# Weights of three stages in one pool, and the mixer's gate product, sum and split in the PSUM bank

## The chip, the core and the metric

The kernel runs on one core of a Trainium2 chip. The metric is the time of one execution on the device in microseconds (us); each kernel's time is the median of several runs. Engines: TensorE (PE; PEld is its weight load), VectorE (DVE), ScalarE (ACT), GpSimd (POOL) and SyncE (SP), which here issues every DMA.

## The reference, cut to what matters

Two transformer blocks over 1024 positions of width 1024, in fp32. The part that the change touches is the first half of block 1:

```python
h = rms_norm(x, g_pre_mix)
q, k, v, cb, cc, cu, ga, gc = split(h @ w_in)
o = stick_breaking_attention(heads(q), heads(k), heads(v))   # 8 heads of 64
y_attn = o @ w_attn_out
y_conv = (cb * causal_depthwise_conv(cc * cu, w_conv)) @ w_conv_out
gate_attn, gate_conv = split(sigmoid([ga, gc] + b_gate))
mixed = (gate_attn * y_attn + gate_conv * y_conv) @ w_o
x = x + rms_norm(mixed, g_post_mix)
...                          # MLP (relu squared, 4096 wide), a gated addition from p,
...                          # then block 2: two attention layers with memory
```

## The kernel before

Activations lie transposed, features on the 128 partitions, and each fp32 matrix product is three matmuls of a wider type: every operand is split in a high part and the rest, and `mm3` (L120 to L126) adds high by high (L124), low by high (L125) and high by low (L126) into one PSUM bank of 128 x 512. A weight tile comes by `split_w` (L89 to L105): SP loads it raw (L103), ACT makes the high part (L104), POOL the low part (L105). An activation is split by `split` (L107 to L113): ACT the high part (L112), DVE the low part (L113). `proj_T` runs `mm3` over the k tiles for one half of 512 positions.

The stages run in the order of `STAGES`. `start` makes the normed input, the convolution branch and its gate, and stores `gate_conv * y_conv` in memory as `sT` (L595 sigmoid, L598 product into `s_yc`, L599 store). `stick` (L601) is the attention: four pairs of heads, for each the weights of k, v and q; to the later pairs a `gate` (L630 on) is added that makes one of the first seven tiles of `gate_attn` (L637, into `ga`, one buffer) and stores it in `gaT` (L638). Gates 5 and 6 run at its end. The attention output goes to memory as `oT`, high and low part (L647, L648). `mix` (L657) makes the eighth gate (weight `w7`, tile `ga7`), reads `oT` back into `oh4` and `ol4` (L679, L680; 16 loads of 256 KB), and for each of eight tiles `m` of the mixed output loads a `w_attn_out` tile, `gaT[m]` into `ga_m` (L686) and `sT[m]` into `s_m` (L687). For each half it multiplies in PSUM bank `ps_y` (12 matmuls), then on DVE `ga = ps_y * ga` (L692) and `ga = ga + s` (L693), then splits `ga` into `act_hi` and `act_lo` (L112, L113). `ps_y` has six banks. Then `out_stage`, whose first matmuls are `r_o` (L760 to L762), with `w_o` as the weight.

`run` (L70) opens the pools. A stage or tuple of stages that stands in a tuple gets `dense` (L79): a pool `w` with two buffers each of `wraw`, `w_hi` and `w_lo`, and a pool `wx` with four more of each part, to which two of three weights go. `stick` opens a pool `w` of its own, without `wx`. Where a pool closes and the next opens at the same addresses, the tiles of the new one wait until those of the old one are released. The order of instructions on each engine is set by a scheduler, from dependences, buffers and its own estimates, not by the order of the code.

Of the kernel before, what the change touches and what calls it, by code (L numbers as in the profile page):

```python
# [13 lines left out]
ALU = mybir.AluOpType  # L14
# [14 lines left out]
class Net:  # L29
# [40 lines left out]
    def run(self, stages):  # L70

        for s in stages:
            with ExitStack() as st:
                if isinstance(s, tuple):
                    self.dense(st)
                for name in (s if isinstance(s, tuple) else (s,)):
                    getattr(self, name)()


    def dense(self, st):  # L80

        self.weights(st)
        self.wx = st.enter_context(self.tc.tile_pool(name="wx", bufs=4))
        st.callback(lambda: setattr(self, "wx", None))

# [515 lines left out]
    def stick(self):  # L601

        nc, tc, a = self.nc, self.tc, self.a
        hi, lo = self.act_hi, self.act_lo
        act = (hi, lo)
        col = lambda k: slice(k * P, (k + 1) * P)
        bg = self.bg
        gaT = self.gaT = self.dram.tile([8, P, S], F32, name="gaT")
        oT = self.oT = self.dram.tile([4, 2, P, S], F32, name="oT")
        with ExitStack() as st:  # L610
            self.weights(st)
            A = self.attn_pools(st, (3, 0, 3, 1, 1), stick=True)
            Ts = {}

            def produce(p):
                def gen():
                    T = Ts[p] = self.pair_tiles(A, p)
                    for gi, what in ((4, "k"), (8, "v"), (0, "q")):
                        w = self.split_w(a["w_in"][gi + p], 1024)
                        for h in range(2):  # L620
                            ps = self.ps_proj(A)
                            self.proj_T(ps, w, col, act, 8, h)
                            if what == "v":
                                self.v_evac(A, ps, T, h)
                            else:
                                self.qk_evac(ps, h, T, what, 0.125 if what == "q" else None, once=True)
                            yield
                return gen

            def gate(m):  # L630
                def gen():
                    w = self.split_w(a["w_in"][24 + m], 1024)
                    for h in range(2):
                        ps = self.ps_proj(A)
                        self.proj_T(ps, w, col, act, 8, h)
                        s = A["pp"].tile([P, H], F32, name="ga", tag="ga", bufs=1)
                        nc.scalar.activation(out=s, in_=ps, func=AF.Sigmoid, bias=bg[:, m:m + 1])  # L637
                        nc.sync.dma_start(out=gaT[m, :, h * H:h * H + H], in_=s)  # L638
                        yield
                return gen  # L640

            def items_of(p):
                def done(c, op, _):
                    oh = A["pp"].tile([P, H], F32R, name="oh", tag="oh", bufs=1)
                    ol = op.bitcast(F32R)
                    self.split(oh, ol, op)
                    nc.sync.dma_start(out=oT[p, 0, :, c * H:c * H + H], in_=oh.bitcast(F32))  # L647
                    nc.sync.dma_start(out=oT[p, 1, :, c * H:c * H + H], in_=ol.bitcast(F32))  # L648
                return self.pair_items(Ts[p], "stick", None, 1.0, done)

            self.run_pairs(A, [(6, produce(p)) for p in range(4)], items_of,
                           [[], [], [(2, gate(0))], [(2, gate(m)) for m in range(1, 5)]])
            for m in (5, 6):
                for _ in gate(m)():
                    pass

    def mix(self):  # L657

        nc, tc, a = self.nc, self.tc, self.a
        hi, lo = self.act_hi, self.act_lo  # L660
        act = (hi, lo)
        col = lambda k: slice(k * P, (k + 1) * P)
        sT, gaT, oT = self.sT, self.gaT, self.oT
        with ExitStack() as st:
            cv = st.enter_context(tc.tile_pool(name="mxo", bufs=1))
            c2 = st.enter_context(tc.tile_pool(name="mx2", bufs=4))
            psm = st.enter_context(tc.tile_pool(name="psmx", bufs=6, space=PSUM))
            oh = cv.tile([P, 4, S], F32R, name="oh4")
            ol = cv.tile([P, 4, S], F32R, name="ol4")
            w7 = self.split_w(a["w_in"][31], 1024)  # L670
            w0 = self.split_w(a["w_attn_out"][0], 512)
            ga7 = cv.tile([P, S], F32, name="ga_7")
            for h in range(2):
                sl = slice(h * H, h * H + H)
                ps = psm.tile([P, H], F32, name="ps_y")
                self.proj_T(ps, w7, col, act, 8, h)
                nc.scalar.activation(out=ga7[:, sl], in_=ps, func=AF.Sigmoid, bias=self.bg[:, 7:8])
                for p in range(4):
                    nc.sync.dma_start(out=oh[:, p, sl].bitcast(F32), in_=oT[p, 0, :, sl])  # L679
                    nc.sync.dma_start(out=ol[:, p, sl].bitcast(F32), in_=oT[p, 1, :, sl])  # L680
            for m in range(8):
                w = self.split_w(a["w_attn_out"][m], 512) if m else w0
                ga = c2.tile([P, S], F32, name="ga_m") if m < 7 else ga7
                s = c2.tile([P, S], F32, name="s_m")
                if m < 7:
                    nc.sync.dma_start(out=ga, in_=gaT[m])  # L686
                nc.sync.dma_start(out=s, in_=sT[m])  # L687
                for h in range(2):
                    sl = slice(h * H, h * H + H)
                    ps = psm.tile([P, H], F32, name="ps_y")  # L690
                    self.proj_T(ps, w, col, (oh, ol), 4, h)
                    nc.vector.tensor_tensor(out=ga[:, sl], in0=ps, in1=ga[:, sl], op=ALU.mult)  # L692
                    nc.vector.tensor_tensor(out=ga[:, sl], in0=ga[:, sl], in1=s[:, sl], op=ALU.add)  # L693
                    self.split(hi[:, m, sl], lo[:, m, sl], ga[:, sl])


    def out_stage(self, wsrc, gpost, gpre, xsrc, xdst, filler=None, after=None, first=(), banks=None):
# [876 lines left out]
                self.out_stage(a["w_out_2"][1], a["norm_post_2"][1:2], None, self.xd, self.a["out"], first=first)  # L1574


STAGES = (("start",), "stick", ("mix", "mlp", "layer_a"), "attn_a", "layer_b")


@with_exitstack  # L1580
def tile_net(ctx: ExitStack, tc: tile.TileContext, args: dict):
    Net(ctx, tc, args).run(STAGES)

# [82 lines left out]
```

## Time and profile before

| | us |
|---|---|
| median of 3 runs | 2939.25 (2936.12 to 2941.45) |
| the profiled execution | 2939.78 |
| its span | 2938.0 |
| mean granted clock of TensorE, of full speed | 0.979 |

In a row of the timeline stand the start in us, the duration, the engine, the line of the kernel, the operation and `out<-in`; in square brackets how long the engine had been idle before it and what ended that. Matmul durations overlap: one of 0.39 us starts 0.23 us after the last at full clock, one of 0.63 us 0.43 us after the last at the lower clock. A row with `xN` covers N instructions in a row.

### The profile page before, as it was taken

How to read it: one execution, taken by the hardware profiler on the slowest of the kernel's cores; microseconds unless marked ns; L12 is line 12 of the kernel's file. 1: busy time of each engine (PE TensorE's matmuls, PEld its weight loads, DVE VectorE, ACT ScalarE, POOL GpSimd, SP SyncE). 2: the span in 40 equal slices, each digit the busy share in tenths (PEclk: the TensorE clock that was granted, in tenths of full speed). 3: DMA queues.
4: the chain of work that ended last, by engine and by line, in shares of the span. 5: the costliest groups of instructions: out<-in, count | busy, mean ns of one | idle time of the engine just before them, and what ended most of it. 6: DMA issues, size and time to landing. Idle time of an engine off the chain costs nothing. (4 is left out here: it accounts for less than half of the span.)

```text
span 2938.0 us, 37990 instructions
## 1 busy us (share of the span) xinstructions
PE 2767.0 (94%) x13490; PEld 2303.1 (78%) x13490; DVE 1684.0 (57%) x3177; ACT 1222.8 (42%) x2403; POOL 985.6 (34%) x826
## 2 busy tenths in 40 slices
PE   7999999997999999999989899699999999999988
PEld 5888778886887887888867789677777988788867
DVE  5420288855387766766577534377872436666643
ACT  5111266643352222211134423377773535555542
POOL 4211111113235543222246312332324344555441
PEclk9999999998999999999999999899999999999999
DMA  5112211117323335332123321543344332222163
GB/s 208 47 43 68 75 46 60 58 61 251 118 97 106 128 109 170 115 105 93 66 71 136 133 94 64 180 122 95 121 137 170 106 117 65 72 72 74 56 204 118
DMA packets 140293, 311.15 MB, mean 106 GB/s; under 512 B 15868, under 2 KB 35964, under 8 KB 140104
## 3 DMA queue, kind: packets, MB, share of 16 engines
q1 hardware_dynamic: 140104, 308.73, 31.4%
q8 instruction: 107, 1.75, 0.2%
q14 instruction: 82, 0.67, 0.1%
HBM read 213.33 MB, written 85.38 MB: 102 GB/s over the span
## 5 line engine op out<-in xcount | busy, mean ns | idle before, releaser
L105 POOL TENSOR_TENSOR w_lo<-w_raw,w_hi 128x1024 fp32r<-128x1024 f32 (+5 forms) x223 | 440.2, 1983 | 1036.0 <-ACT w_hi L104 1021.5
L104 ACT ACTIVATE w_hi<-w_raw 128x1024 fp32r<-128x1024 f32 (+5 forms) x223 | 193.0, 877 | 407.3 <-PE ps L125 90.6
L124 PE MATMUL ps_m<-act_hi,w_hi 128*128 128x512 f32 x716 | 287.2, 401 | 22.6 <-DVE qb L343 6.3
L125 PE MATMUL ps_m<-act_lo,w_hi 128*128 128x512 f32 x716 | 281.4, 393 | 0.0
L126 PE MATMUL ps_m<-act_hi,w_lo 128*128 128x512 f32 x716 | 280.7, 393 | 0.2
L113 DVE TENSOR_TENSOR pl<-tp_at,ph 128x512 fp32r<-128x512 f32 (+3 forms) x416 | 222.9, 561 | 84.0 <-ACT ph L112 81.8
L112 ACT ACTIVATE ph<-tp_at 128x512 fp32r<-128x512 f32 (+3 forms) x416 | 196.7, 500 | 107.6 <-PE tp_at L304 96.4
L304 PE MATMUL tp_at<-ident,p 128*128 128x128 f32 x1280 | 204.9, 275 | 18.0 <-DVE pl L113 6.5
L259 ACT ACTIVATE p<-p,mx 128x256 f32<-128x256 f32 (+7 forms) x256 | 180.2, 706 | 74.5 <-DVE mx L248 41.6
L1037 DVE TENSOR_TENSOR acc<-ps_d,acc 128x512 f32<-128x512 f32 x240 | 161.5, 687 | 82.1 <-PE ps_d L126 82.1
L124 PE MATMUL ps_d<-w_hi,act_hi 128*128 128x512 f32 x512 | 200.3, 391 | 2.8 <-DVE f_out L890 1.3
L125 PE MATMUL ps_d<-w_lo,act_hi 128*128 128x512 f32 x512 | 199.5, 390 | 0.0
L126 PE MATMUL ps_d<-w_hi,act_lo 128*128 128x512 f32 x512 | 199.5, 390 | 0.0
L304 PEld LDWEIGHTS tp_at<-ident,p 128*128 128x128 f32 x1280 | 152.6, 141 | 50.6 <-DVE pl L113 9.2
L124 PEld LDWEIGHTS ps_m<-act_hi,w_hi 128*128 128x128 f32 x716 | 135.3, 189 | 58.3 <-PE s_ps L226 8.8
L760 PE MATMUL r_o<-w_hi,act_hi 128*128 128x512 f32 x384 | 152.0, 399 | 12.4 <-DVE ga L692 8.0
L126 PEld LDWEIGHTS ps_m<-act_hi,w_lo 128*128 128x128 f32 x716 | 134.7, 188 | 29.3 <-POOL w_lo L105 1.3
L125 PEld LDWEIGHTS ps_m<-act_lo,w_hi 128*128 128x128 f32 x716 | 135.3, 189 | 25.5
L296 PE MATMUL o_ps<-ph,v 128*128 128x512 f32 (+3 forms) x400 | 146.5, 367 | 6.3 <-ACT ph L112 3.3
L762 PE MATMUL r_o<-w_hi,act_lo 128*128 128x512 f32 x384 | 151.9, 396 | 0.0
L761 PE MATMUL r_o<-w_lo,act_hi 128*128 128x512 f32 x384 | 151.6, 396 | 0.0
L297 PE MATMUL o_ps<-pl,v 128*128 128x512 f32 (+3 forms) x400 | 147.6, 377 | 0.4 <-DVE pl L113 0.2
(393 smaller groups left out, 6930.1 us busy)
## 6 DMA issues: line engine op xcount, KB each, us to landing
w_raw<-in_w_in SPq DMA_DIRECT2D x40, 512.0 KB, 3.5
w_raw<-in_w_up SPq DMA_DIRECT2D x32, 512.0 KB, 3.6
f_rows_up<-f_out SPq DMA_DIRECT2D x64, 256.0 KB, 2.4
f_raw<-f_rows_up SPq DMA_DIRECT2D x64, 256.0 KB, 2.6
w_raw<-in_w_down SPq DMA_DIRECT2D x32, 512.0 KB, 4.5
xd<-x_o SPq DMA_DIRECT2D x16, 512.0 KB, 2.8
x_o<-xd SPq DMA_DIRECT2D x16, 512.0 KB, 10.6
w_raw<-in_w_out SPq DMA_DIRECT2D x13, 512.0 KB, 5.2
```

What stands on the lines that cost most here:

```text
L104: nc.scalar.activation(out=hi[:, sl], in_=raw, func=AF.Copy)
L105: nc.gpsimd.tensor_tensor(out=lo[:, sl], in0=raw, in1=hi[:, sl].bitcast(F32), op=ALU.subtract)
L112: nc.scalar.activation(out=hi, in_=src, func=AF.Copy)
L113: nc.vector.tensor_tensor(out=lo, in0=src, in1=hi.bitcast(F32), op=ALU.subtract)
L124: nc.tensor.matmul(out, lhsT=sh, rhs=mh, start=(i == 0), stop=False)
L125: nc.tensor.matmul(out, lhsT=sh, rhs=ml, start=False, stop=False)
L126: nc.tensor.matmul(out, lhsT=sl, rhs=mh, start=False, stop=(i == n - 1))
L259: nc.scalar.activation(out=p[:, :nk], in_=p[:, :nk], func=AF.Exp, scale=-1.0, bias=mx[:, 0:1], accum_out=it["sum"][:, j:j + 1])
L304: nc.tensor.transpose(tp[:, j * P:(j + 1) * P], it["p"][j][:, k * P:(k + 1) * P], self.ident)
L760: nc.tensor.matmul(r, lhsT=a, rhs=wh, start=(k == 0), stop=False)
L762: nc.tensor.matmul(r, lhsT=b, rhs=wh, start=False, stop=(k == 7))
L1037: nc.vector.tensor_tensor(out=acc[:, t, sl], in0=ps, in1=acc[:, t, sl], op=ALU.add)
```

## The change

`STAGES` nests `start`, `stick` and the tuple `("mix", "mlp", "layer_a")` in one tuple, and `run` opens the pool `w` once for it. `stick` no longer opens one. `wx` is opened by the new `ahead` for an inner tuple alone, so for `start` and for `mix` to `layer_a`, as before. In `mix`, product and sum are written to the bank `ps` and the split reads it; `ga` and `s` are only read. The number of instructions of each kind and engine stays the same.

```diff
@@ run
                 if isinstance(s, tuple):
-                    self.dense(st)
-                for name in (s if isinstance(s, tuple) else (s,)):
-                    getattr(self, name)()
+                    self.weights(st)
+                for d in (s if isinstance(s, tuple) else (s,)):
+                    with ExitStack() as more:
+                        if isinstance(d, tuple):
+                            self.ahead(more)
+                        for name in (d if isinstance(d, tuple) else (d,)):
+                            getattr(self, name)()
@@ dense
         self.weights(st)
+        self.ahead(st)
+
+    def ahead(self, st):
         self.wx = st.enter_context(self.tc.tile_pool(name="wx", bufs=4))
@@ stick
         with ExitStack() as st:
-            self.weights(st)
             A = self.attn_pools(st, (3, 0, 3, 1, 1), stick=True)
@@ mix
-                    nc.vector.tensor_tensor(out=ga[:, sl], in0=ps, in1=ga[:, sl], op=ALU.mult)
-                    nc.vector.tensor_tensor(out=ga[:, sl], in0=ga[:, sl], in1=s[:, sl], op=ALU.add)
-                    self.split(hi[:, m, sl], lo[:, m, sl], ga[:, sl])
+                    nc.vector.tensor_tensor(out=ps, in0=ps, in1=ga[:, sl], op=ALU.mult)
+                    nc.vector.tensor_tensor(out=ps, in0=ps, in1=s[:, sl], op=ALU.add)
+                    self.split(hi[:, m, sl], lo[:, m, sl], ps)
@@ end
-STAGES = (("start",), "stick", ("mix", "mlp", "layer_a"), "attn_a", "layer_b")
+STAGES = ((("start",), "stick", ("mix", "mlp", "layer_a")), "attn_a", "layer_b")
```

Lines of the changed kernel are numbered 7 higher from `dense` to `stick`, 6 higher from there on: L104 is L111, L113 is L120, L692 is L698.

The order moves at three places. ACT from `start` to `stick` (`s_yc` is the last work of `start`; `ka` is the first result of `stick`; each `w_hi` here is a weight of `stick`), before:

```order
L595 ACTIVATE s_yc<-ps,bg 128x512 x6
L104 ACTIVATE w_hi<-w_raw 128x1024 x2
L337 ACTIVATE ka_2110<-ps_m_2119 128x512
L104 ACTIVATE w_hi<-w_raw 128x1024
L337 ACTIVATE ka_2110<-ps_m_2150 128x512
```

and now:

```order
L602 ACTIVATE s_yc<-ps,bg 128x512 x3
L111 ACTIVATE w_hi<-w_raw 128x1024
L602 ACTIVATE s_yc<-ps,bg 128x512 x3
L111 ACTIVATE w_hi<-w_raw 128x1024
L344 ACTIVATE ka_2106<-ps_m_2115 128x512
L111 ACTIVATE w_hi<-w_raw 128x1024
```

The first weight of `stick` stands three activations earlier; its load on SP and its L105 on POOL have moved with it.

SP from `stick` to `mix` (`oT` and `gaT` are the stores of `stick`; `in_w_in` the weight `w7`), before:

```order
L638 DMA gaT<-ga 128x512 x2
L647 DMA oT<-oh 128x512
L648 DMA oT<-opair 128x512
L638 DMA gaT<-ga 128x512
L103 DMA w_raw<-in_w_in 128x1024
L103 DMA w_raw<-in_w_attn_out 128x512
L638 DMA gaT<-ga 128x512
L679 DMA oh_5409<-oT 128x512
L680 DMA ol_5410<-oT 128x512
```

and now (the load of `w7` stands five rows ahead of these):

```order
L644 DMA gaT<-ga 128x512 x2
L653 DMA oT<-oh 128x512
L654 DMA oT<-opair 128x512
L110 DMA w_raw<-in_w_attn_out 128x512 x2
L644 DMA gaT<-ga 128x512
L110 DMA w_raw<-in_w_attn_out 128x512 x3
L644 DMA gaT<-ga 128x512
L110 DMA w_raw<-in_w_attn_out 128x512
L685 DMA oh_5401<-oT 128x512
L686 DMA ol_5402<-oT 128x512
```

Seven of eight `w_attn_out` loads stand before the first `oh` load, one of them before these rows; before it was one of eight, and the other seven stood among the loads of `ga_m` and `s_m`. On PE the 48 `w7` matmuls, which stood behind the last gate, now stand 23 between its halves and 25 behind it.

DVE at the end of `mix` (`ga_5423` is `ga7`; L777 is the first work on `r_o`), before:

```order
L692 TENSOR_TENSOR ga_m<-ps_y,ga_m 128x512
L693 TENSOR_TENSOR ga_m<-ga_m,s_m 128x512
L113 TENSOR_TENSOR act_lo<-ga_m,act_hi 128x512 x2
L692 TENSOR_TENSOR ga_5423<-ps_y,ga_5423 128x512
L693 TENSOR_TENSOR ga_5423<-ga_5423,s_m 128x512
L113 TENSOR_TENSOR act_lo<-ga_5423,act_hi 128x512
L692 TENSOR_TENSOR ga_5423<-ps_y,ga_5423 128x512
L693 TENSOR_TENSOR ga_5423<-ga_5423,s_m 128x512
L113 TENSOR_TENSOR act_lo<-ga_5423,act_hi 128x512
```

and now:

```order
L120 TENSOR_TENSOR act_lo<-ps_y,act_hi 128x512
L699 TENSOR_TENSOR ps_y<-ps_y,s_m 128x512
L698 TENSOR_TENSOR ps_y<-ps_y,ga_5415 128x512
L120 TENSOR_TENSOR act_lo<-ps_y,act_hi 128x512
L699 TENSOR_TENSOR ps_y<-ps_y,s_m 128x512
L120 TENSOR_TENSOR act_lo<-ps_y,act_hi 128x512
L783 TENSOR_TENSOR r_5854<-r_o,gpost 128x512 x8
```

The three passes of a tile are the same; the last product now stands ahead of the split of the tile before it. The last reader of a `ps_y` bank is now the split.

The lists also differ at the tail of the MLP (1490 to 1680 us of the trace), where the down projection's rows are normed (`rstd_y`), scaled (L1012, L991) and transposed on PE (`tp`, split by L112 and L113), and the gate matmuls `ps_pg` run. ACT there, before:

```order
L1004 ACTIVATE junk_f,ss<-acc 128x1024 x2
L112 ACTIVATE act_hi<-tp 128x4x128
L1012 ACTIVATE acc<-acc,rstd_y 128x512
L991 ACTIVATE xn<-acc,rstd_y 128x512
L112 ACTIVATE act_hi<-tp 128x4x128
L104 ACTIVATE w_hi<-w_raw 128x1024
```

and now:

```order
L1010 ACTIVATE junk_f,ss<-acc 128x1024 x2
L119 ACTIVATE act_hi<-tp 128x4x128 x2
L111 ACTIVATE w_hi<-w_raw 128x1024
L1018 ACTIVATE acc<-acc,rstd_y 128x512
L997 ACTIVATE xn<-acc,rstd_y 128x512
L1056 ACTIVATE g_p<-ps_pg 128x512
```

The second split of the pair and one weight stand ahead of the scaling that follows `rstd_y`.

## Rows read from the trace of the kernel before

**Rows 1.** The page, part 1: busy time of each engine, share of the span, instructions.

```profile
PE 2767.0 (94%) x13490; PEld 2303.1 (78%) x13490; DVE 1684.0 (57%) x3177; ACT 1222.8 (42%) x2403; POOL 985.6 (34%) x826
```

**Rows 2.** Timeline of PE, start to stick: start us, us, operation, [idle before <-releaser].

```profile
324.73 0.79 PE L124 MATMUL ps_m<-act_hi,w_hi 128*128 128x512 f32 x1 [5.61 <-ACT w_hi L104]
...
328.73 0.57 PE L124 MATMUL ps_m<-act_hi,w_hi 128*128 128x512 f32 x1
329.14 0.40 PE L125 MATMUL ps_m<-act_lo,w_hi 128*128 128x512 f32 x1
```

**Rows 3.** Timeline of the other engines at the same place.

```profile
319.19 0.81 SPq L103 DMA_DIRECT2D w_raw<-in_w_in  x2
319.23 0.69 DVE L598 TENSOR_TENSOR s_yc<-ps,s_yc 128x512 f32<-128x512 f32 x1 [7.21 <-PE ps L126]
...
323.62 1.06 ACT L104 ACTIVATE w_hi<-w_raw 128x1024 fp32r<-128x1024 f32 x1 [6.54 <-DMA w_raw<-in_w_in]
...
324.75 2.37 POOL L105 TENSOR_TENSOR w_lo<-w_raw,w_hi 128x1024 fp32r<-128x1024 f32 x1 [53.26 <-ACT w_hi L104]
```

**Rows 4.** Busy us by stretch: PE, PEld, DVE, ACT, POOL; then PEclk, DMA share, GB/s.

```profile
654.00:661.00 7.00, 6.05 (x26) 4.43 (x24) 0.00 (x0) 0.73 (x2) 0.00 (x0) 1.00 0.10 37
...
670.00:680.00 10.00, 10.00 (x36) 8.12 (x37) 0.00 (x0) 0.69 (x1) 0.00 (x0) 0.81 0.99 344
```

**Rows 5.** Timeline of PE, stick to mix.

```profile
655.14 0.50 PE L124 MATMUL ps_m<-act_hi,w_hi 128*128 128x512 f32 x1 [0.83 <-ACT ga L637]
...
666.14 0.80 PE L124 MATMUL ps_y<-act_hi,w_hi 128*128 128x512 f32 x1 [5.26 <-ACT w_hi L104]
...
682.09 0.39 PE L125 MATMUL ps_y<-ol,w_hi 128*128 128x512 f32 x1
```

**Rows 6.** Timeline of SP, stick to mix.

```profile
661.84 0.38 SPq L638 DMA_DIRECT2D gaT<-ga  x1
666.41 0.33 SPq L679 DMA_DIRECT2D oh<-oT  x1
...
677.26 0.32 SPq L680 DMA_DIRECT2D ol<-oT  x1
```

**Rows 7.** The tile ol, 645 to 700 us: from issue to landing.

```profile
DMA to landing us min/median/max: 3.7/5.8/7.9
```

**Rows 8.** Timeline of all engines in mix, 702 to 708 us.

```profile
702.52 3.08 POOL L105 TENSOR_TENSOR w_lo<-w_raw,w_hi 128x512 fp32r<-128x512 f32 x2 [3.35 <-ACT w_hi L104]
...
703.83 0.69 DVE L692 TENSOR_TENSOR ga_m<-ps_y,ga_m 128x512 f32<-128x512 f32 x1 [0.78 <-PE ps_y L126]
...
704.43 1.71 DVE L113 TENSOR_TENSOR act_lo<-ga_m,act_hi 128x512 fp32r<-128x512 f32 x1
...
706.07 0.68 DVE L693 TENSOR_TENSOR ga_m<-ga_m,s_m 128x512 f32<-128x512 f32 x1
```

**Rows 9.** Groups by form, 660 to 735 us: xcount | busy us, mean ns | idle before.

```profile
L113 DVE TENSOR_TENSOR act_lo<-ga_m,act_hi 128x512 fp32r<-128x512 f32 x14 | 15.8, 1132 | 3.7 <-ACT act_hi L112 3.4
L693 DVE TENSOR_TENSOR ga_m<-ga_m,s_m 128x512 f32<-128x512 f32 x14 | 13.7, 979 | 0.2
...
L692 DVE TENSOR_TENSOR ga_m<-ps_y,ga_m 128x512 f32<-128x512 f32 x14 | 9.6, 686 | 36.1 <-PE ps_y L126 36.1
```

**Rows 10.** Timeline of all engines, mix to r_o.

```profile
725.16 0.39 PE L126 MATMUL ps_y<-oh,w_lo 128*128 128x512 f32 x1
725.29 3.43 DVE L113 TENSOR_TENSOR act_lo<-ga_m,act_hi 128x512 fp32r<-128x512 f32 x2
...
733.55 0.76 PE L760 MATMUL r_o<-w_hi,act_hi 128*128 128x512 f32 x1 [8.01 <-DVE ga L692]
...
738.77 0.39 PE L760 MATMUL r_o<-w_hi,act_hi 128*128 128x512 f32 x1
```

**Rows 11.** Timeline of all engines, tail of the MLP.

```profile
1541.68 0.72 ACT L1012 ACTIVATE acc<-acc,rstd_y 128x512 f32<-128x512 f32 x1 [6.17 <-DVE rstd_y L163]
...
1543.75 1.12 PE L183 MATMUL tp<-ident,xn 128*128 128x128 f32 x4 [5.83 <-DVE act_lo L113]
```

## Prediction, made before the changed kernel ran

> **What bounds the kernel now.** The page's first part comes first: TensorE is busy for 2767.0 us of the span of 2938.0, 94%, DVE, the next to compute, for 57% [rows 1]. Time can therefore go only where TensorE stands idle or runs at the lower of its clocks; work taken from ACT, DVE or POOL is worth nothing by itself. So the waits of TensorE are read next, as the timeline prints them behind a row, at the places where the order of instructions differs between the two kernels. Those are three: the hand-over from `start` to `stick`, the hand-over from `stick` to `mix` with all of `mix`, and the tail of the MLP (1490 to 1680 us). Between them each engine's list is the same row for row.
>
> At the first hand-over TensorE is idle for 5.61 us and then runs at the lower clock (starts 0.41 us apart at its end, where 0.227 is normal, below) until 329.14 [rows 2]. It waits for ACT's `w_hi`, whose raw weight SP asked for only at 319.19, as the old weight pool closed; it came 4.4 us later [rows 3]. At the second, the same takes 5.26 us at 666.14 [rows 5], and 8.01 us stand at the end of `mix`, at 733.55 [rows 10]. Those are 19 of the 171 us in which TensorE is idle.
>
> **Part 1: one pool, start to stick.** The new order puts the first weight of `stick` (load, L104, L105) and the next two loads ahead of the last three `s_yc` activations. So `w_hi` and `w_lo` (2.37 us on POOL, idle there for 53 us) are ready before 319, and the first `ps_m` matmul waits only for the reader of the last bank of `start`, DVE's 0.69 us from 319.23, which ends at 319.92 [rows 3]. I put its start at 320.0 in place of 324.73: −4.7. The idle time left, some 0.9 us, should not lower the clock: 0.83 us at 655.14 did not, with a granted clock of 1.00 in that stretch [rows 4, 5]. At full clock the 11th matmul then starts at 320.0 + 10 × 0.23 = 322.3, where it was 329.14: **−6.8 us**, or −4.7 if the clock falls all the same. Nothing new is late: a weight feeds 48 matmuls, 10.9 us, so the second is due at 331 and the third at 342, and ACT comes to the second right behind the last `s_yc`, at about 319.3, POOL's 2.37 us behind that.
>
> **Part 2: one pool, stick to mix.** The `w7` weight and seven of the eight `w_attn_out` weights now load while `stick` ends; SP no longer waits there for a pool to close. The 48 `w7` matmuls stand no longer behind the last gate but around it: 23 fall between its two halves, so the 0.83 us for the single `ga` buffer goes as well. From 654.3, where the first half ends [rows 5], 24 gate matmuls and 48 of `w7` take 72 × 0.227 = 16.3 us (0.227 is the distance of the 190 starts from 682.09 to 725.16 [rows 5, 10]). `w7` is done at 670.7; it was at 682.09: −11.4.
>
> That gain is not all kept. The attention outputs `oh4` and `ol4` must still be read back, by 16 loads: first issue 666.41, last 677.26, median landing 5.8 us, so 683.1, or 16.7 us from first issue to last landing [rows 6, 7]. The first stands behind the last `gaT` store, and that store now comes after a gate half that ends at 654.3 + 47 × 0.227 = 665.0, where it was 660.9. The store held the loads for 4.6 us (661.84 to 666.41 [rows 6]); if it does so again, from 666, they start at 670.6, and if it lands in 2 us, at 668. I take 668.6, as fewer weights compete with it. The loads then end at 685.3. TensorE trickles from 670.7 on, and has done two of 16 output tiles by the last landing; the other 168 matmuls take 38.1 us. TensorE's part of `mix` ends at about 723 in place of 725.6: of the 11.4 us only 2 to 3 are kept, because memory (0.99 of the DMA engines at 670 to 680 [rows 4]) is the bound of this stretch. The trickle may also cost a stretch at the lower clock, about 2 us as at 324.73; that is left to the range.
>
> **Part 3: product, sum and split in the bank.** The counts stay: three DVE passes a tile, one of ACT. Before, the product L692 reads the bank and SBUF, and the sum L693 and L113 read SBUF twice. Under POOL's L105 the latter stretch and the former does not: within the 3.08 us from 702.52 L692 took 0.69 and L113 1.71, and L693 was back at 0.68 behind it [rows 8]; over 14 tiles the means are 686 ns, 979 and 1132 [rows 9]. Now each of the three has an operand in the bank. I take 0.69 for each, by L692; the other end is L113's 1.13, since no row shows DVE writing its result to a bank.
>
> [...]
>
> What it adds: a bank is free only after L113, not after L692. TensorE fills a tile in 12 × 0.227 = 2.72 us, six banks are in use, and DVE needs 3 × 0.69 = 2.07 a tile: no wait in steady state. At the end it pays. Before, DVE was behind when the last matmul ended: 3.43 us for two L113 from 725.29, then the last two tiles, and `r_o` started 8.0 us after TensorE's end [rows 10]. Now product, sum, ACT's pass and split of the last tile remain, with one split of the tile before among them: 4 × 0.69 + 0.63 + hand-overs of 0.5 = 3.9 us. The price is that the banks of `r_o` wait for the last split, where they waited for the last product. `r_o` starts at 723 + 3.9 = 726.9, not 733.55: **−6.6 us for parts 2 and 3 together**; −10 with loads that end some 3 us sooner, −3 with loads from 670.6 and the lower clock. That `r_o` starts at the lower clock (fast again from 738.77 [rows 10]) I leave as it is: 3.9 us is near the 5.6 that did it at 324.73.
>
> **Part 4: the tail.** By no line of the diff, the order also shifts where the MLP ends: some `tp` transposes stand a few matmuls later, some L112 and L113 ahead of L1012 and its kin, one L105 earlier on POOL. At 1543.75 TensorE waits 5.83 us for `act_lo`: ACT's L112 stood behind an L1012 that itself waited 6.17 us for `rstd_y` [rows 11]. In the new list this L112 passes it. So that wait can shrink, and one for `xn` can take its place, as DVE makes `xn` behind the same `rstd_y`. The ends are −6 (gone) and +6 (once more elsewhere). I take **−1.3**, near nothing, since the chain of `rstd_y` is as long as before.
>
> Sum: −6.8 − 6.6 − 1.3 = −14.7. Against the profiled execution of 2939.78 us, 0.5 above the median of 2939.25, that is 2925.1: **2925 us**.
>
> **The rivals.** (a) *The loads eat part 2.* The store holds them 4.6 us, they end at 687.3, TensorE at 725 with some 2 us at the lower clock: `r_o` at about 730.5, −3; the whole −11, 2928 to 2930. For it: DMA at 0.99. Against: fewer weights in the queue.
> (b) *The held banks bind.* The three passes stretch as L113 did, 3 × 1.13 = 3.4 us a tile; from 2.72 on DVE falls behind, here by 16 × 0.68 = 10.9, and the end takes 5.5: `r_o` at 739, +6 in place of −6.6, so −2 in all, 2937. Against: L692's mean.
> (c) *The tail gives more.* The 5.83 us and some 2 of lower clock go: about 2918.
> (d) *Slower: the tail turns against us.* `tp` waits for `xn` behind `rstd_y`, 5.83 + 2 us each time. Two such waits cancel the 13.4 us of the hand-overs; three give +23.5 − 13.4, 2949. For it: the tail has eight such chains. Against: the moved `tp` stand behind more matmuls, not fewer.
> (e) *It does not do what it says*: the loads come no earlier, 2939. The order speaks against it.
>
> **How the numbers follow.** Forecast (2921 to 2928) 0.50; (a) 0.17; (b) 0.09; (c) 0.16; (d) 0.05; (e) 0.03. 0.2%, 5.9 us, is about what a measurement of this kernel can tell from no change, so faster is below 2933.4: the forecast, (a) and (c), 0.83. (b) and (e) are the same, 0.12; (d) is slower, 0.05. The range is 2914 to 2937: it takes in (a), (b) and (c) with their bounds and leaves out (d), (e) and the far ends.
>
> **What would show it.** Right: `ps_m` near 320 with no slow matmuls behind it; `w7` among the gate's matmuls; idle time before the first `oh` matmuls near 671 to 674; L113 of `mix` at 0.69 under POOL; `r_o` about 4 us after the last `ps_y`. Wrong: waits of `ps_y` for L113 (b); new waits of `tp` after 1500 us (d), or old ones gone (c); `oh` loads issued after 670 (a).

## The result

The changed kernel takes 2914.84 us (median of 4 runs, 2912.21 to 2916.28), the kernel before, beside it, 2940.12: a ratio of 0.9912, 95% interval 0.9898 to 0.9926, so 25 us less. The prediction was 2925 (2914 to 2937), faster. Direction, range and the mechanism of the first part hold; the gain is 1.7 times the 14.7 us forecast. In a second group of runs the same kernel came to 2921.62 (6 runs, 2912.80 to 2922.98) against 2942.48: 0.9922, interval 0.9905 to 0.9938. So the gain is 21 to 25 us, 1.4 to 1.7 times the forecast.

The page's first part, answering to [rows 1]:

```profile
PE 2757.3 (95%) x13490; PEld 2297.5 (79%) x13490; DVE 1678.1 (58%) x3177; ACT 1220.9 (42%) x2403; POOL 982.5 (34%) x826
```

TensorE's busy time fell by 9.7 us, the span by 27.6 (2938.0 to 2910.4): 18 us of waiting went, and some 10 us more that TensorE had spent on the same 13490 matmuls, because some of them ran at the lower clock: TensorE's mean granted clock is 0.979 before and 0.984 now.

**Where the 27.6 us are.** Both traces hold the same matmuls, so the start of the first matmul of a named group dates each stage. The table has, for all kernels of this study, how much shorter (-) each stage is than in the kernel before: *start* from the first matmul to the last of `start`; *hand-over* from there to the first `s_ps`; *mixer* to the first `ps_f` (so with the rest of `stick`, `mix` and most of `r_o`); *MLP* to the first `ps_pg`; *tail* to the first `ps_mem`; *block 2* to the last `r_o`. Each row is one profiled execution, its first column the median against the kernel before in the same group of runs.

| kernel | median | start | hand-over | mixer | MLP | tail | block 2 |
|---|---|---|---|---|---|---|---|
| changed | -25.3 | -0.8 | -6.8 | -10.6 | -0.3 | -6.3 | -2.7 |
| changed, again (e10) | -20.9 | +1.1 | -6.8 | -10.0 | +0.1 | -6.0 | +3.7 |
| e1, pool alone | -17.9 | -0.8 | -6.8 | -10.8 | +0.1 | -3.1 | -2.2 |
| e2, bank alone | -0.4 | 0.0 | +0.1 | -2.7 | -0.9 | +3.5 | -0.4 |
| e3, bank, pool start to stick | -13.6 | +1.3 | -6.8 | -2.7 | -1.0 | -2.5 | -2.8 |
| e4, bank, pool from stick on | -16.5 | -0.4 | -0.1 | -12.6 | +0.6 | -6.3 | -1.8 |
| e5, gate 6 in the mixer | -15.4 | +1.8 | -6.8 | -16.2 | +2.3 | -3.1 | +6.3 |
| e6, shared banks | -14.6 | +1.0 | -6.8 | -14.9 | +0.8 | +4.3 | +3.5 |
| e7, both | -19.2 | +1.1 | -6.8 | -18.4 | +1.9 | -3.1 | +6.6 |
| e8, two banks (1 run) | -11.4 | -1.0 | -6.8 | +0.6 | +0.8 | -6.0 | +1.1 |
| e9, gate 6, its weight in `w` | -30.1 | +1.1 | -6.8 | -16.9 | -0.9 | -3.3 | -3.4 |
| e11, half the read-back (1 run) | -22.8 | +1.8 | -6.8 | -16.3 | +1.5 | -4.4 | +3.5 |
| e12, e9 with the SBUF mixer | -22.4 | +0.2 | -6.8 | -12.4 | -1.5 | -2.4 | +3.2 |

The two rows of the changed kernel show what one execution can tell: hand-over, mixer and tail repeat within 0.6 us, but start differs by 1.9 and block 2 by 6.4, with the same instructions in the same order. e4, whose order from `stick` on is the changed kernel's too, has 12.6 in the mixer, so two to three us there tell nothing either. Block 2 and start are not read as effects of anything here. What repeats is 6.8 + 10.3 + 6.2 = 23.3 us, and the two medians lie on either side of it.

**The first hand-over** in the changed kernel, timeline of all engines, answering to [rows 2, 3]:

```profile
318.15 1.06 ACT L111 ACTIVATE w_hi<-w_raw 128x1024 fp32r<-128x1024 f32 x1 [1.89 <-PE ps L132]
...
319.15 0.50 PE L131 MATMUL ps_m<-act_hi,w_hi 128*128 128x512 f32 x1 [0.85 <-DVE s_yc L605]
...
319.49 0.39 PE L132 MATMUL ps_m<-act_lo,w_hi 128*128 128x512 f32 x1
```

`w_hi` is made while `start` still runs, the idle time is 0.85 us on the last reader of its bank, and the next matmul starts 0.34 us later, those behind it at 0.23: no lower clock.

**Stick to mixer.** SP's issues and the landing of the `ol` tile, answering to [rows 6, 7], then TensorE:

```profile
658.30 0.33 SPq L644 DMA_DIRECT2D gaT<-ga  x1
...
660.36 0.33 SPq L685 DMA_DIRECT2D oh<-oT  x1
...
669.74 0.32 SPq L686 DMA_DIRECT2D ol<-oT  x1
```

```profile
DMA to landing us min/median/max: 5.3/5.4/5.4
```

```profile
662.49 0.39 PE L133 MATMUL ps_y<-act_hi,w_lo 128*128 128x512 f32 x1
665.07 0.47 PE L131 MATMUL ps_y<-oh,w_hi 128*128 128x512 f32 x1 [2.19 <-DMA ol<-oT]
...
666.47 0.80 PE L131 MATMUL ps_y<-oh,w_hi 128*128 128x512 f32 x1 [0.46 <-DMA oh<-oT]
...
672.50 0.51 PE L131 MATMUL ps_y<-oh,w_hi 128*128 128x512 f32 x1
```

The first issue comes 2.06 us behind the last `gaT` store (4.6 before); the last load lands at about 669.74 + 5.4 = 675.1 (the trace tells the landing of two of the eight `ol` loads). TensorE is through with `w7` at 662.9, waits 2.19 us, then 0.46, and runs at the lower clock for 13 matmuls, from 666.47 to 672.50 (not 17, as the expectation of e5 has it). The busy times by stretch, answering to [rows 4], say the same: granted clock 0.70, DMA at 0.99:

```profile
662.00:672.00 10.00, 7.35 (x19) 4.50 (x18) 0.00 (x0) 1.20 (x2) 1.26 (x1) 0.70 0.99 340
```

**The mixer's passes and its end**, groups by form from 640 to 730 us and the timeline of all engines, answering to [rows 8 to 10]:

```profile
L699 DVE TENSOR_TENSOR ps_y<-ps_y,s_m 128x512 f32<-128x512 f32 x16 | 10.9, 691 | 0.4 <-DMA s_m<-sT 0.4
...
L120 DVE TENSOR_TENSOR act_lo<-ps_y,act_hi 128x512 fp32r<-128x512 f32 x16 | 10.7, 682 | 1.4 <-ACT act_hi L119 1.3
```

```profile
709.33 2.40 POOL L112 TENSOR_TENSOR w_lo<-w_raw,w_hi 128x1024 fp32r<-128x1024 f32 x1 [1.52 <-ACT w_hi L111]
...
710.63 0.68 DVE L120 TENSOR_TENSOR act_lo<-ps_y,act_hi 128x512 fp32r<-128x512 f32 x1
...
716.13 0.47 PE L766 MATMUL r_o<-w_hi,act_hi 128*128 128x512 f32 x1 [3.43 <-DVE act_lo L120]
...
717.14 0.63 PE L767 MATMUL r_o<-w_lo,act_hi 128*128 128x512 f32 x1
```

Each of the 48 passes takes 0.68 to 0.70 us, under POOL's L112 too (710.63 lies within 709.33 + 2.40). `r_o` starts 3.43 us after TensorE's last `ps_y` matmul. Its first four matmuls still run at full clock, then eight at the lower one; before, twelve did.

**The tail of the MLP.** Two waits that the prediction did not name, in the kernel before, TensorE and then ACT:

```profile
1643.15 1.06 PE L183 MATMUL tp<-ident,xn 128*128 128x128 f32 x4 [3.85 <-DVE act_lo L113]
...
1669.87 1.31 PE L183 MATMUL tp<-ident,xn_m 128*128 128x128 f32 x8 [3.89 <-issue]
```

```profile
1641.74 0.72 ACT L991 ACTIVATE xn<-acc,rstd_y 128x512 f32<-128x512 f32 x1 [5.14 <-DVE rstd_y L163]
```

and TensorE and ACT in the changed kernel, answering to [rows 11]:

```profile
1525.73 0.80 PE L133 MATMUL ps_pg<-w_hi,act_lo 128*128 128x512 f32 x1 [5.51 <-DVE act_lo L120]
...
1623.95 0.66 PE L190 MATMUL tp<-ident,xn 128*128 128x128 f32 x4 [1.02 <-DVE rstd_u L168]
...
1627.67 1.31 PE L190 MATMUL tp<-ident,xn 128*128 128x128 f32 x8 [1.42 <-DVE act_lo L120]
...
1646.60 1.06 PE L190 MATMUL tp<-ident,xn_m 128*128 128x128 f32 x8 [2.52 <-issue]
```

```profile
1620.94 1.06 ACT L119 ACTIVATE act_hi<-tp 128x512 fp32r<-128x512 f32 x2
...
1625.68 0.72 ACT L997 ACTIVATE xn<-acc,rstd_y 128x512 f32<-128x512 f32 x1 [1.77 <-DVE rstd_y L170]
```

The 5.83 us of [rows 11] are still there, as 5.51 in front of a `ps_pg` matmul. Gone is the later 3.85, with 1.02 and 1.42 in its place: the splits of the pair (1620.94) now stand ahead of an L997 that waits for `rstd_y` (1625.68), where before the split stood behind an L991 that had waited 5.14 us. The last wait fell from 3.89 to 2.52. But of the 6.3 us only 1.7 are shorter waits (18.4 us of idle time in the tail before, 16.8 now); the other 4.6 are matmuls that no longer run at the lower clock. In the busy times of one stretch, first before, then changed, the granted clock is 0.91 and 1.00:

```profile
1630.00:1650.00 20.00, 16.15 (x75) 13.10 (x73) 14.59 (x30) 10.55 (x17) 11.09 (x7) 0.91 0.35 132
```

```profile
1612.00:1632.00 20.00, 17.50 (x87) 13.74 (x86) 15.92 (x31) 11.93 (x20) 10.15 (x6) 1.00 0.37 139
```

### The profile page after: what moved, and what is told of

Its sections match the earlier page's. It is cut to its first block, busy times and chain, and to the rows that moved or that the text cites. A ratio compares the mean times of both kernels' runs of the same rounds, so it can differ in the third digit from the quotient of the medians.

```text
span 2910.4 us, 37974 instructions
## 1 busy us (share of the span) xinstructions
PE 2757.3 (95%) x13490; PEld 2297.5 (79%) x13490; DVE 1678.1 (58%) x3177; ACT 1220.9 (42%) x2403; POOL 982.5 (34%) x826
## 5 line engine op out<-in xcount | busy, mean ns | idle before, releaser
L112 POOL TENSOR_TENSOR w_lo<-w_raw,w_hi 128x1024 fp32r<-128x1024 f32 (+5 forms) x223 | 438.8, 1977 | 1015.2 <-ACT w_hi L111 1011.8
L111 ACT ACTIVATE w_hi<-w_raw 128x1024 fp32r<-128x1024 f32 (+5 forms) x223 | 193.2, 877 | 401.0 <-PE ps L132 99.7
L131 PE MATMUL ps_m<-act_hi,w_hi 128*128 128x512 f32 x716 | 286.1, 400 | 16.9 <-DVE qb L350 6.5
L120 DVE TENSOR_TENSOR pl<-tp_at,ph 128x512 fp32r<-128x512 f32 (+3 forms) x416 | 222.7, 560 | 85.4 <-ACT ph L119 83.2
```

The source lines that it names most:

```text
L111: nc.scalar.activation(out=hi[:, sl], in_=raw, func=AF.Copy)
L112: nc.gpsimd.tensor_tensor(out=lo[:, sl], in0=raw, in1=hi[:, sl].bitcast(F32), op=ALU.subtract)
L120: nc.vector.tensor_tensor(out=lo, in0=src, in1=hi.bitcast(F32), op=ALU.subtract)
L131: nc.tensor.matmul(out, lhsT=sh, rhs=mh, start=(i == 0), stop=False)
```

## The experiments

Theory after the result: three gains that have nothing to do with each other, 6.8 us from the weights that come before `stick`, 10 from what comes before and in the mixer, 6 from a new order in the tail. Rivals: the gains overlap; the bank part is what matters in the mixer; the tail's gain is a chance of one execution.

**e1: the pool alone.** The mixer's three lines as before.

```diff
-                    nc.vector.tensor_tensor(out=ps, in0=ps, in1=ga[:, sl], op=ALU.mult)
-                    nc.vector.tensor_tensor(out=ps, in0=ps, in1=s[:, sl], op=ALU.add)
-                    self.split(hi[:, m, sl], lo[:, m, sl], ps)
+                    nc.vector.tensor_tensor(out=ga[:, sl], in0=ps, in1=ga[:, sl], op=ALU.mult)
+                    nc.vector.tensor_tensor(out=ga[:, sl], in0=ga[:, sl], in1=s[:, sl], op=ALU.add)
+                    self.split(hi[:, m, sl], lo[:, m, sl], ga[:, sl])
```

> The one pool alone; product, sum and split of the mixer in SBUF as before. Theory: the hand-over start to stick still gives -6.8 us, and TensorE's part of the mixer still ends some 13 us earlier than before, but product and sum stretch again under GpSimd's weight splits (mean of L113 near 1.1 us in place of 0.69), so r_o starts 2 to 5 us later than in the changed kernel: 2917 to 2920 if the tail of the MLP is worth the same. Rival (the bank part gives nothing, since r_o then waits for a product and not for a split): r_o 1 to 3 us earlier than in the changed kernel, 2912 to 2914.

Measured: 2921.74 us, ratio 0.9940 (0.9920 to 0.9960). DVE's groups in its mixer, and the start of `r_o`:

```profile
L699 DVE TENSOR_TENSOR ga_m<-ga_m,s_m 128x512 f32<-128x512 f32 x14 | 15.8, 1145 | 0.4 <-DMA s_m<-sT 0.4
```

```profile
714.73 0.77 PE L766 MATMUL r_o<-w_hi,act_hi 128*128 128x512 f32 x1 [3.83 <-ACT act_hi L119]
...
720.22 0.69 DVE L120 TENSOR_TENSOR act_lo<-ga,act_hi 128x512 fp32r<-128x512 f32 x1 [0.70 <-ACT act_hi L119]
```

L699 is stretched as the theory has it (1145 ns), and yet `r_o` starts at 714.73, 1.4 us earlier than in the changed kernel. It does not wait for the last split, which is done only at 720.9, still before `r_o` needs it; the last product ends at 714.58, and ACT's `act_hi`, which the row names, at 714.64. Up to `ps_f` pool alone and changed kernel are equal (-10.8, -10.6). So the rival is right in the mixer: with the pool, the bank part gives nothing there that the traces can tell. The whole is above both ranges expected: 17.9 us below the kernel before, against 25.3 and 20.9, with intervals that overlap. In the traces 3 us of that are in the tail, which has another order here and the same idle time (16.8 us), so I put them down to the clock, an estimate.

**e2: the bank alone.** The three lines of the change in the kernel before.

```diff
-                    nc.vector.tensor_tensor(out=ga[:, sl], in0=ps, in1=ga[:, sl], op=ALU.mult)
-                    nc.vector.tensor_tensor(out=ga[:, sl], in0=ga[:, sl], in1=s[:, sl], op=ALU.add)
-                    self.split(hi[:, m, sl], lo[:, m, sl], ga[:, sl])
+                    nc.vector.tensor_tensor(out=ps, in0=ps, in1=ga[:, sl], op=ALU.mult)
+                    nc.vector.tensor_tensor(out=ps, in0=ps, in1=s[:, sl], op=ALU.add)
+                    self.split(hi[:, m, sl], lo[:, m, sl], ps)
```

> Product, sum and split in the bank alone; pools as before. Theory: both waits for the first weight (5.6 and 5.3 us) stay, all three DVE passes take 0.69 under GpSimd, r_o starts 3.4 us after the last matmul of the mixer in place of 8.0: -4 to -5 there, and the tail of the MLP, whose order differs from both kernels, gives -6 to +6: 2935 (2929 to 2941). Rival (held banks cost): waits of ps_y for the split appear and r_o comes no earlier: 2940.

Measured: 2939.23 us, ratio 0.9999 (0.9990 to 1.0009). The end of its mixer:

```profile
726.67 1.06 ACT L104 ACTIVATE w_hi<-w_raw 128x1024 fp32r<-128x1024 f32 x1 [3.05 <-DMA w_raw<-in_w_o]
727.63 0.58 ACT L112 ACTIVATE act_hi<-ps_y 128x512 fp32r<-128x512 f32 x1
...
731.59 0.76 PE L760 MATMUL r_o<-w_hi,act_hi 128*128 128x512 f32 x1 [5.65 <-DVE act_lo L113]
```

Here the bank part gives 2.7 us in the mixer, not 4 to 5: `r_o` starts 5.65 us after the last matmul, since ACT took a weight (L104, 726.67), for whose load it had waited 3.05 us, ahead of the split that the chain needed. Its tail, in another order again, gives it back: the long wait now stands there twice (3.64 and 5.72), and the one of 3.85 stayed.

```profile
1538.94 0.79 PE L126 MATMUL ps_pg<-w_hi,act_lo 128*128 128x512 f32 x1 [3.64 <-DVE act_lo L113]
...
1554.04 0.79 PE L126 MATMUL ps_pg<-w_hi,act_lo 128*128 128x512 f32 x1 [5.72 <-DVE act_lo L113]
...
1642.28 0.66 PE L183 MATMUL tp<-ident,xn 128*128 128x128 f32 x4 [3.83 <-DVE act_lo L113]
```

**e3 and e4: the pool over one hand-over each**, with the bank part.

```diff
-STAGES = ((("start",), "stick", ("mix", "mlp", "layer_a")), "attn_a", "layer_b")
+STAGES = ((("start",), "stick"), (("mix", "mlp", "layer_a"),), "attn_a", "layer_b")    # e3
+STAGES = ((("start",),), ("stick", ("mix", "mlp", "layer_a")), "attn_a", "layer_b")    # e4
```

> Bank part, and one pool over start and stick only; the mixer opens its own. Theory: -6.8 at the first hand-over as in the changed kernel, the 5.3 us wait for w7 back, so the run before it less 6.8: 2928 (2922 to 2934). Rival (the first gain is given back later, since stick is paced by something else than TensorE): no faster than the bank part alone, 2935.

> Bank part, and one pool over stick and the stages behind it only; start has its own. From stick on its instruction order is that of the changed kernel on every engine, so only the first hand-over differs. Theory: 5.6 us of waiting and some 2 us at the lower clock come back and nothing else: 2921.7, 6.8 above the changed kernel (6 to 8). Rival (the gains overlap): within 3 us of the changed kernel.

Measured: e3 2926.05 us, 0.9951 (0.9936 to 0.9965); e4 2923.16, 0.9941 (0.9925 to 0.9958). The stages separate cleanly: e3 has the whole 6.8 at the first hand-over and e2's 2.7 in the mixer; e4 has nothing at the first and all of the mixer (12.6, which is 2 us more than the changed kernel in the same order). The gains do not overlap, and e4's 16.5 plus 6.8 is the 23.3 of above. e3 is 13.2 us faster than e2, not 6.8: the other 6.0 are in the tail (+3.5 and -2.5), whose order in e3 is, but for two rows of TensorE, that of the changed kernel.

**e5: gate 6 in the mixer.** If the read-back sets the pace between 662 and 672 us, more matmuls that do not need it should hide it.

```diff
-            for m in (5, 6):
+            for m in (5,):
                 for _ in gate(m)():
...
-            w7 = self.split_w(a["w_in"][31], 1024)
+            wg = {m: self.split_w(a["w_in"][24 + m], 1024) for m in (6, 7)}
...
-            ga7 = cv.tile([P, S], F32, name="ga_7")
-            for h in range(2):
+            gas = {m: cv.tile([P, S], F32, name=f"ga_{m}") for m in (6, 7)}
+            for m, h in ((6, 0), (6, 1), (7, 0), (7, 1)):
```

> The changed kernel, and gate 6 moves from the end of stick into the mixer beside gate 7, kept in SBUF: its store to memory and its load fall away, and the attention outputs can be read back while 96 gate matmuls (21.8 us) run. Theory (in the changed kernel the read-back sets the pace between 662 and 672 us): the waits of 2.2 and 0.5 us for it and the 17 matmuls at the lower clock behind them go, 5 to 6 us up to the start of r_o. The tail of the MLP gets a third order, worth -3 to +9 against the changed kernel: 2910 (2906 to 2918). Rival (the read-back is hidden already): r_o no earlier.

Measured: 2924.57 us, 0.9953 (0.9937 to 0.9970). TensorE's two longest waits from 640 to 740 us (us in total, times, longest):

```profile
PE r_o L766 <- DVE act_lo L120: 3.4, 1, 3.4
PE ps_y L131 <- ACT w_hi L111: 2.1, 1, 2.1
```

and the first load of the read-back on SP:

```profile
650.65 0.32 SPq L685 DMA_DIRECT2D oh<-oT  x1
```

No wait for the read-back is left, and the mixer is 5.6 us shorter than in the changed kernel, as expected. All 16 loads are still there, but the first goes out 12.6 us earlier, counted from the first `s_ps`, as no `gaT` store of gate 6 stands ahead of it. The total is a miss: 10 us above the changed kernel's first group, 5 above the second. Behind the mixer the MLP (+2.3) and the tail (-3.1 in place of -6.3) give back 5.8 us, both in another order; block 2 is longer too (+6.3), which with its spread is not read.

**e6: the mixer's banks shared with what follows.** One pool of six banks, opened ahead of `mix` and closed behind `mlp`; `ps_y` takes the tag of `r_o`.

```diff
-            psm = st.enter_context(tc.tile_pool(name="psmx", bufs=6, space=PSUM))
+        self.hold = ExitStack()
+        self.pm = psm, _ = (self.hold.enter_context(tc.tile_pool(name="psf", bufs=6, space=PSUM)),
+                            self.hold.enter_context(tc.tile_pool(name="pstf", bufs=2, space=PSUM)))
...
-                    ps = psm.tile([P, H], F32, name="ps_y")
+                    ps = psm.tile([P, H], F32, name="ps_y", tag="r")
```

> The changed kernel, with one set of six banks for the mixer and all that follows it, so that r_o takes the bank of a tile that was split long ago. Theory (r_o waits for the last split only because its pool opens on the mixer's banks): the wait of 3.4 us before r_o and the eight matmuls at the lower clock behind it go, -4 to -5 up to r_o's second half: 2910, and the tail may give some of it back. Rival (r_o needs the last split as its operand): r_o no earlier, 2915.

Measured: 2925.42 us, 0.9952 (0.9938 to 0.9967). `r_o` behind the last `ps_y`, and a wait of its tail:

```profile
715.26 0.39 PE L133 MATMUL ps_y<-oh,w_lo 128*128 128x512 f32 x1
715.49 0.39 PE L768 MATMUL r_o<-w_hi,act_hi 128*128 128x512 f32 x1
```

```profile
1537.47 0.79 PE L133 MATMUL ps_pg<-w_hi,act_lo 128*128 128x512 f32 x1 [6.99 <-DVE act_lo L120]
```

`r_o` follows without a gap and at full clock: 4.3 us in the mixer, as the theory has it. The tail took 10.6 us more than the changed kernel's, in the order of e2 and with the same three waits, one of them longer (3.62, 6.99 and 3.87 us; e2 has 3.64, 5.72 and 3.83). The total is a miss by it (2910 expected).

**e7, both:**

> Both of the above. If the two waits are separate, -9 to -11 up to r_o's second half, 2905 with a tail as in the changed kernel, up to 2914 with a tail as in the kernel with the bank part alone. Rival (one takes the other's place): no better than the better of the two.

Measured: 2920.82 us, 0.9936 (0.9922 to 0.9951). The mixer is 7.8 us shorter than in the changed kernel, less than the sum of 9.9. The total is a miss (2905 to 2914 expected): as in e5, the MLP (+1.9) and the tail (-3.1) give part of it back.

**e8: two banks.** `bufs=2` in place of 6 for `psmx`.

> The changed kernel with two banks for the mixer in place of six. A bank is held for 3.4 to 3.9 us after its last matmul (product, sum, ScalarE's half, split), and a tile takes TensorE 2.72 us, so with two banks TensorE waits 0.7 to 1.2 us a tile, 10 to 18 us in all; with six it has 13.6 us and no wait. Rival (the in-place passes already bind with six): 0.7 to 1.2 us a tile is far exceeded, over 25 us.

Measured: 2928.60 us, one run; the mixer takes 11.2 us more than in the changed kernel. A wait of TensorE in it, and its busy times further on:

```profile
680.50 0.79 PE L131 MATMUL ps_y<-oh,w_hi 128*128 128x512 f32 x1 [4.12 <-DVE act_lo L120]
```

```profile
692.00:702.00 10.00, 10.00 (x42) 7.46 (x43) 7.31 (x11) 3.91 (x5) 2.40 (x1) 1.00 0.82 270
```

So the price is in the range expected, but only partly as expected: 4.1 us and a stretch at the lower clock (0.63 us a matmul up to 685.78) fall on the first tiles, and 42 or 43 matmuls in 10 us, for 46 at full pace, on the others. With six banks no such wait was found.

**e9: e5 with the order kept.** `split_w` counts its calls, and two of three go to `wx`; moving a weight from `stick` to `mix` turned that count for all later ones. Here gate 6's weight goes to `w` without being counted, and the order of all computing engines from the end of the mixer on is that of the changed kernel. **e10** is the changed kernel beside it. The edit against e5:

```diff
-            wg = {m: self.split_w(a["w_in"][24 + m], 1024) for m in (6, 7)}
+            wg = {m: self.split_w(a["w_in"][24 + m], 1024,
+                                  room=(self.w, "w_hi", "w_lo") if m == 6 else None) for m in (6, 7)}
```

> Gate 6 in the mixer as before, but its weight goes to the pool w and so does not turn the count by which two of three weights go to wx. From the end of the mixer on, the order on every engine is that of the changed kernel. Theory (what e5 gained up to r_o, 5.6 us, it lost again only by another order of the MLP's tail and of block 2): 5 to 6 us below the changed kernel run beside it, 2909; the tail as in the changed kernel. Rival (an earlier start is lost behind r_o whatever the order): the changed kernel's time.

> The changed kernel itself, again, beside the others of this group: 2915 (2911 to 2919), and a second look at its tail of the MLP: the same waits, 5.5 us for act_lo and 1.0 and 1.4 in place of 3.85, so some 6 us below the kernel before between the first gate matmul and the end of the tail. Rival (the tail's gain was the chance of one execution): 0 to 2 us there.

Measured: e9 2912.35 us (2909.77 to 2912.60), 0.9896 (0.9876 to 0.9916); e10 2921.62, 0.9922 (0.9905 to 0.9938). e9 is 9.3 us below e10, and every run of it below every run of e10, by 0.2 us at the closest. Against the kernel before it is 30.1 below, the changed kernel 25.3 and 20.9, so the total gains 5 to 9 us, for 5 to 6 expected; e10 itself came out above its range (2911 to 2919). In the traces 6.9 us are the mixer, the tail takes 2.7 back, and 7.1 stand in block 2, which is not read. TensorE waits once in the mixer:

```profile
PE r_o L766 <- DVE act_lo L120: 4.0, 1, 4.0
```

e10's tail repeats the changed kernel's (-6.0, -6.3), so its gain is no chance of one execution. e9's tail, in the same order, gives only 3.3. Of the 2.7 us between them 1.1 are waits, the longest of 1.63 us for `act_lo` where e10 has 1.05, with ACT waiting 1.08 us for a weight ahead of it. The other 1.6 are clock, behind the last wait of the tail, in e9 and then in e10:

```profile
1643.28 1.06 PE L190 MATMUL tp<-ident,xn_m 128*128 128x128 f32 x8 [2.41 <-issue]
...
1645.55 0.63 PE L131 MATMUL ps_ad<-act_hi,w_hi 128*128 128x512 f32 x1
```

```profile
1650.51 1.06 PE L190 MATMUL tp<-ident,xn_m 128*128 128x128 f32 x8 [2.48 <-issue]
...
1652.35 0.39 PE L131 MATMUL ps_ad<-act_hi,w_hi 128*128 128x512 f32 x1
```

Over all kernels the tail occurs in four orders. That of the kernel before is the zero of the table; that of e2 and e6 gives +3.5 and +4.3; that of e1, e5, e7, e11 and e12 gives -2.4 to -4.4; that of the changed kernel, with e3, e4, e8, e9 and e10, gives -2.5 to -6.3. So the order goes with a loss or a gain, and within one order the tail still moves by up to 3.8 us. No run changed the order of the tail alone.

**e11: half the read-back.** The eight `ol` loads are left out and `oh` is used in their place.

```diff
-                    nc.sync.dma_start(out=ol[:, p, sl].bitcast(F32), in_=oT[p, 1, :, sl])
...
-                    self.proj_T(ps, w, col, (oh, ol), 4, h)
+                    self.proj_T(ps, w, col, (oh, oh), 4, h)
```

> The changed kernel without the eight reads of the attention output's low part (the high part's tile stands in for it in the matmuls, so that part of the sum is left out). Theory (the read-back sets the pace from 662 to 672 us): half the bytes, the last matmul of the mixer 3 to 5 us earlier. Rival (the first load's own delay sets it, not the bytes): under 1 us.

Measured: 2919.65 us, one run. TensorE's waits from 640 to 740 us:

```profile
PE r_o L764 <- DVE act_lo L120: 3.4, 1, 3.4
PE ps_m L131 <- ACT ga L643: 0.4, 1, 0.4
```

and the first load of the read-back and the last `gaT` store on SP:

```profile
644.26 0.32 SPq L684 DMA_DIRECT2D oh<-oT  x1
...
663.95 0.33 SPq L644 DMA_DIRECT2D gaT<-ga  x1
```

The wait for the read-back is gone and the mixer is 5.7 us shorter, even more than expected, so the read-back did set that stretch. Whether by its bytes or by its start the run does not tell, for the order on SP moved too: the first load stands 19.7 us ahead of the last `gaT` store, where in the changed kernel it stands 2.06 us behind it. e5 and e9, which read all the bytes, have no wait either once the loads start early enough; so an earlier start is enough, and the rival, which put the delay to the start, is not refuted.

**e12: e9 with product, sum and split in SBUF.** The lines of e1 in e9.

> As e9, with product, sum and split in SBUF as before. With six banks and the pool the bank part gave nothing up to the second half of r_o, since DVE had slack while TensorE waited for the read-back. Here TensorE does not wait, so DVE's stretched passes (mean about 1.1 us) could bind: theory, r_o's second half and what follows 1 to 3 us later than in e9 (mixer's matmuls unhindered, the end of the mixer longer). Rival (DVE hides it as before): no later. The tail has the order of the run with the pool alone, 3 us above e9's: 2913 to 2916.

Measured: 2920.09 us, 0.9924 (0.9906 to 0.9941), and 4.5 us longer than e9 in the mixer. TensorE's wait at its end, and the mean of the split:

```profile
PE r_o L766 <- ACT act_hi L119: 8.0, 1, 8.0
```

```profile
L120 DVE TENSOR_TENSOR act_lo<-ga_m,act_hi 128x512 fp32r<-128x512 f32 x12 | 14.3, 1194 | 6.1 <-ACT act_hi L119 5.6
```

8.0 us against e9's 4.0, and DVE has no pause over 0.1 us from 704.45 to the last product at 714.58. Here DVE binds, and the bank part pays what it did not pay in e1. The 4.5 us are more than the 1 to 3 expected. The total, above its range as well (2913 to 2916), also holds 6.6 us of block 2.

## Why the prediction was right, and where it was off

**Part 1** was right to 0.1 us: 0.85 us of idle time, no lower clock, -6.8; in all eleven traces with that pool the stage gives 6.8, in the two without it 0.1 or less.

**Part 2** had the right chain and too large a term. Moved by the 7.66 us that stand between the two traces at the first `s_ps`, the changed kernel has `w7` done at 670.5 (forecast 670.7), the first read-back issued at 668.0 (668.6), the last landing at 682.8 (685.3), TensorE's last `ps_y` matmul over at 720.4 (723) and `r_o` at 723.8 (726.9). The mis-sized term is the 16.7 us from first issue to last landing: it measured 14.8, of which issuing is 9.4 (10.9 before) and the landing 5.4 (5.8 before, the middle of two loads that took 3.7 and 7.9). No weight is issued between the first and the last of them in either kernel, so why they went faster stays open. The stretch at the lower clock, which I left to the range, is there (granted clock 0.70 from 662 to 672 us of its own trace).

**Part 3.** 0.69 us a pass was right, and 3.9 us to `r_o` measured 3.4. Wrong was the credit: I took the 8.0 us at the end of the mixer as what the bank part removes. e1 has 3.8 us there with the old passes, so about half of it goes with the pool alone. DVE's sums are stretched more there than before (means of 1145 and 979 ns) and its splits less (838 and 1132), but its order is another: the last product stands ahead of the split before it (713.89 and 714.67), where before it stood behind (732.73 and 730.75). No run separates order and passes there. In the mixer the bank part is worth 2.7 us without the pool, nothing that the traces can tell with it, 4.5 in e9. That `r_o` starts at the lower clock as before was also wrong: eight matmuls in place of twelve, 0.8 us. Part 2 and 3 together: -10.6 and -10.0 for -6.6, near the far end that I gave.

**Part 4** was wrong in place and in size: -6.3 and -6.0 for -1.3. I bounded one wait, of 5.83 us, and that one stayed. The waits of 3.85 and 3.89 at the end of the same stretch, which stood in the same list of TensorE's waits, I did not cost, nor the lower clock behind them. The end of -6 that I gave was reached by another way. That is luck. The errors, some 4 us in parts 2 and 3 and 5 us here, lie on the same side, and the first group's 2914.84 is only 0.84 us inside the end of the range.

Of the rivals, (a) did not happen as such, since the loads came at 668.0; (b) is refuted by the passes at 0.68 to 0.70 and by e8; (c), the tail gives more, came true in size, but through other waits than the one of 5.83 us and through the clock; (d) did not happen in the changed kernel, but in e2 and e6 the tail does turn against the change, by 3.5 and 4.3 us, with waits for `act_lo` and not for `xn`.

## What to carry to other kernels

A pool that stays open over a stage's end is worth the idle time at that end plus the matmuls at the lower clock behind it, as long as no other wait takes its place: at the first hand-over that came out to a tenth of a microsecond, at the second the read-back took part of it. Faster passes of an engine pay only where that engine is late: the same edit gave 0, 2.7 and 4.5 us in the mixer, by what TensorE waited for beside it. Where a scheduler sets the order, cost every wait of each stretch whose order differs, not the longest alone, and judge a local change by its own stage as well as by the total: e5 gained 5.6 us where it was made and gave all of it back behind it; with one uncounted weight and the old order, e9 came out 5 to 9 us below the changed kernel. An experiment must also be read for what else it moved: e11 was to halve the bytes of the loads and moved their start as well.

## What the runs showed of the hardware

DVE with one operand in PSUM took 0.68 to 0.70 us for 128 x 512, whether its result went to PSUM or to SBUF, and was not stretched while POOL worked; with both operands in SBUF the sum and the split on `ga_m` had means of 0.84 to 1.19 us in e1 and e12. In the mixer of the kernel before, passes with both operands in SBUF that started while POOL's L105 ran took 0.73 to 2.88 us (2.88 at 715.68, beside L105 from 712.82 to 718.02); those that started while it did not took 0.68 to 0.69, and the product L692, with its operand in PSUM, 0.68 to 0.69 in both cases. So under no POOL work a PSUM operand cost nothing that shows. Why the passes with both operands in SBUF stretch beside POOL no run shows.

The length of a wait alone did not decide TensorE's clock behind it. After 3.43 us of idle time before `r_o` the changed kernel ran four matmuls at the full clock before the lower one set in; after 3.4 us at the same place e5 ran all at the full clock (0.39 us each from the second on); after 3.83 us in e1 and 5.65 in e2 the first was already slow (0.77 and 0.76 us). In the tail the clock fell after 2.41 us in e9 and stayed after 2.48 in e10. What makes the difference stays open, as does the spread of 6.4 us of block 2 between two executions in the same order.
